# Two-layer encoder trunk on one core: plain products for the first two gate/up tiles of each layer, row sums from rows read back, and moved stores, loads and norms

## The chip, the cores and the metric

The kernel runs on 1 core of one Trainium2 chip. The metric is the device time of one execution in microseconds (us); lower is better. In the profile PE is the matmul engine, PEld its weight loads, DVE the vector engine, ACT the scalar engine, POOL the general engine, SP the engine that issues DMAs in this kernel.

## What is computed

Two layers over x of 1024 rows by 1024 columns in float32. Each layer has a mixer (attention heads and an output projection), a layer norm, a gated feed-forward net of width 2816, and a second layer norm:

```
for layer in range(2):
    mix = mixer(x)                                  # attention, output projection
    x = layer_norm(ALPHA * x + mix, ln1_g, ln1_b)   # over the 1024 columns of a row
    g, u = x @ w_gate, x @ w_up                     # 1024 x 2816 each
    x = layer_norm(ALPHA * x + (silu(g) * u) @ w_down, ln2_g, ln2_b)
```

## The kernel before

Rows are handled in 8 tiles of 128 (`tt`, 0 to 7), features in tiles of 128 on the partitions. Every matmul operand is split into a high and a low part (`split`, L105 on ACT and L106 on DVE, `hilo` calls it), and `mm3` (L127) issues three matmuls for one product of 128x128 by 128x512. So a "product" below, a contraction over 512, is 4 x 3 = 12 matmuls.

The feed-forward net is multiplied in 2x2 blocks by a scheme with 7 block products in place of 8. For gate and up (`gate_up`, 22 tiles `f` of 128 features, taken in pairs `j`, `j + 11`) block row 1 or 2 is gate or up, and the transposed rows give blocks: `b11`, `b21` are the two halves of the columns for rows 0 to 3, `b12`, `b22` those for rows 4 to 7, and `t1` to `t4` are differences of such blocks. On the weight side `prep` builds `s1` to `s4` out of the four loaded blocks `a11` to `a22`. A tile's work is `head` (a11 by b11) and `gate0` (a12 by b21), `m6` (s2 by t2) and `tail` (the other four products). `hidden` stores each tile's result and sums of them to DRAM, and `down_sums` loads four blocks of the down weights, subtracts, and stores four sums. `down` then forms seven products over 11 tiles `j`, each with four banks (`bank_a`: 3 pd and 1 pv; `bank_b`: 2 ps and 2 pt), its operands loaded by `parts` (L430, L431) and split.

What sets the order: a program plans the instruction order of every engine ahead of time from the order of the source, the readiness of operands and a model of durations; the engines then work through their lists in order. The source order is thus a wish. In the result an instruction that waits holds up all behind it on its engine. Tiles come from pools with a fixed number of buffers (g 30, s 3, t 11, wh 6, wr 3, h 6; PSUM pd 3, ps 2, pt 2, pv 1).

Around the change. `out_proj` makes the rows one after another and calls `push` (in `ln_pipe`) for each. `push(tt)` does statistics of row `tt` (L153, L155 on DVE, `rstd` L144 and L146 on POOL), scales the row before (L162 DVE, L163 ACT, times gamma L164 on POOL), adds beta to the row before that (L200 DVE), stores it and calls `turn`. The last two rows take a shorter path (L193, four half-row operations on DVE). In the first norm of a layer `turn` transposes rows 0 to 3 (L235) into b11 and b21 and puts off rows 4 to 7: `sums` (L252) builds b22 and t1 to t4 from the rows in SBUF, called from `gate_up` between four early `head`s that only need b11 and b21. In `down`, rows are loaded again from DRAM (L456) and scaled by ALPHA on ACT (L457) after the first product, `push` for rows 0 to 3 stands behind the fifth product (s2 by t2), and in layer 0 `turn` is `ln_turn` (L172), which transposes rows for the next mixer into PSUM tiles of the same pool `pt` that the sixth product (s3 by t3) takes two of. The last product (a22 by t4) has all 11 operand pairs split first, then runs row by row in the source. SP issues every DMA.

Of the kernel before, what the change touches and what calls it, by code (L numbers as in the profile page):

```python
# [39 lines left out]
class Core:  # L40
# [36 lines left out]
    def w(self):  # L77
        return self.whp.tile([P, 2, WC], F32R, tag="wh", name=self.nm("wh"))

# [78 lines left out]
    def ln_scale(self, y, stats, g):  # L158
# [5 lines left out]
        nc.gpsimd.tensor_tensor(y, y, g, op=ALU.mult)  # L164
# [13 lines left out]
    def ln_pipe(self, y, g, b, turn, done):  # L178
# [3 lines left out]
        n = TT - 2  # L182

        def push(tt):
            if 0 <= tt - 1 < n:
                self.ln_scale(y[tt - 1], st[tt - 1], g)
            if tt < TT:
                st[tt] = self.ln_stats(y[tt])
            if n <= tt < TT:
                mv, r = st[tt]  # L190
                for op, s, row in ((ALU.subtract, mv[:, 0:1], g), (ALU.mult, r, b)):
                    for o in (slice(0, 512), slice(512, D)):
                        nc.vector.scalar_tensor_tensor(y[tt][:, o], y[tt][:, o], s, row[:, o], op0=op,  # L193
                                                       op1=ALU.mult if row is g else ALU.add)
                        if row is b:
                            done(tt, y[tt][:, o], o)
            z = tt - 2
            if 0 <= z < TT:
                if z < n:
                    nc.vector.tensor_tensor(y[z], y[z], b, op=ALU.add)  # L200
                    done(z, y[z])
                if turn is not None:
                    turn(z)
# [37 lines left out]
    def turn_sums(self, y, xb, later):  # L241
        nc = self.nc

        def sums(tt):
            a, b = slice(0, 512), slice(512, D)
            x, z = y[tt - 4], y[tt]
            ta, tb = self.s(), self.s()
            t1, t2, t3, t4 = ta[:, a], ta[:, b], tb[:, a], tb[:, b]
            self.turn_block(xb, "b22", z[:, b], tt)
            for name, o, p, q in (("t1", t1, z[:, a], x[:, a]), ("t2", t2, z[:, b], t1),  # L250
                                  ("t3", t3, z[:, b], z[:, a]), ("t4", t4, x[:, b], t2)):
                nc.vector.tensor_tensor(o, p, q, op=ALU.subtract)  # L252
                self.turn_block(xb, name, o, tt)

        def turn(tt):
            if tt < 4:
                self.turn_block(xb, "b11", y[tt][:, 0:512], tt)
                self.turn_block(xb, "b21", y[tt][:, 512:D], tt)
            else:
                later.append(lambda: sums(tt))  # L260
# [1116 lines left out]
```

## Time and profile before

| | us |
|---|---|
| median of 3 runs | 2545.47 (2544.58 to 2548.05) |
| the profiled execution | 2547.79 |
| its span, first to last instruction | 2546.0 |
| PE busy in it | 2381.7 (94%) |
| DVE busy in it | 1657.1 (65%) |

The stages by time in the span: mixer of layer 0 to about 445 us, its output projection to 491, gate/up to 966, down to 1207; mixer of layer 1 to about 1795, its output projection to 1842, gate/up to 2313, down to 2524, last norm to 2546. A busy share is an average over stages with different limits, so each stage is read for itself. A view by stretches gives the busy time of each engine in a stretch, with the number of its instructions after x, and the clock granted to PE (1.00 is 2.4 GHz, 0.50 is 1.2 GHz).

### The profile page before, as it was taken

Reading aid. Unit: us, or ns where it says so; the run is one execution under the profiler, and the core shown is the slowest. Engines: PE = TensorE matmul, PEld = TensorE weight load, DVE = VectorE, ACT = ScalarE, POOL = GpSimd, SP = SyncE. Lnnn points to the kernel's source line nnn. Section 1 sums busy time; section 2 is a strip of 40 time slices with the busy share of each in tenths; the row PEclk is TensorE's granted clock in tenths of the full one; section 3 lists DMA queues with packets and bytes.
Section 4 is the critical chain, followed back from the end, with each engine's and each line's share of the span. In section 5 each row is a group of like instructions: output and inputs, shape, how many; then the busy total and the mean of one; then the engine's idle time right before and its main releaser. Section 6 shows DMA issues by size and latency. Waiting matters only on the chain.

```text
span 2546.0 us, 35845 instructions
## 1 busy us (share of the span) xinstructions
PE 2381.7 (94%) x11912; PEld 1988.3 (78%) x11912; DVE 1657.1 (65%) x3566; ACT 1123.6 (44%) x2292; POOL 598.0 (23%) x966
## 2 busy tenths in 40 slices
PE   8998999889999999969899999999879999999996
PEld 7977887667888887858688888878758788887885
DVE  3577756868677764566546565656768677764567
ACT  5476756342323325334346665554442232324342
POOL 3532455500000000021344654354600000000012
PEclk9999999989999999979899999999979999999998
DMA  4235232325454469314121212141325544459632
GB/s 155 87 101 158 76 112 65 124 83 180 161 162 157 158 231 360 106 61 176 63 79 42 71 44 63 44 147 53 132 80 176 166 154 161 170 169 378 209 110 86
DMA packets 190906, 337.88 MB, mean 133 GB/s; under 512 B 22392, under 2 KB 48376, under 8 KB 190720
## 3 DMA queue, kind: packets, MB, share of 16 engines
q1 hardware_dynamic: 190720, 335.58, 40.1%
q8 instruction: 95, 1.56, 0.3%
q14 instruction: 91, 0.75, 0.1%
HBM read 236.89 MB, written 94.40 MB: 130 GB/s over the span
## 4 chain that ended last, share of the span: by engine, by line
PE 73%; DVE 12%; DMA 7%; ACT 4%; issue 3%; POOL 2%; SPq 1%; DVEq 0%; ACTq 0%; POOLq 0%
PE pd L127 42%; PE ps L127 12%; PE pt L127 7%; PE pv L689 3%; PE pt L678 3%; PE pv L127 2%; DMA wr<-in_wgu 2%; DVE g L106 2%; DMA g<-in_wd 1%; DVE wh L106 1%; DVE s L650 1%; DVE g L200 1%; PE ps L718 1%; DVE g L193 1%; PE ps L719 1%
## 5 line engine op out<-in xcount | busy, mean ns | idle before, releaser
L127 PE MATMUL pd<-g,wh 128*128 128x512 f32 (+1 forms) x2940 | 738.9, 400 | 31.6 <-ACT g L105 8.1
L127 PEld LDWEIGHTS pd<-g,wh 128*128 128x128 f32 (+1 forms) x2940 | 546.7, 190 | 159.0 <-ACT g L105 9.7
L144 POOL TENSOR_SCALAR m<-m 128x1 f32<-128x1 f32 x32 | 16.8, 525 | 1294.8 <-DVE m L155 1293.3
L106 DVE TENSOR_TENSOR wh<-g,wh 128x1024 fp32r<-128x1024 f32 x138 | 173.3, 1260 | 163.7 <-ACT wh L105 148.8
L105 ACT CAST g<-s 128x512 fp32r<-128x512 f32 x192 | 116.7, 621 | 334.7 <-PE pd L127 147.8
L105 ACT CAST wh<-g 128x1024 fp32r<-128x1024 f32 x138 | 145.0, 1053 | 199.6 <-PE pt L127 63.7
L105 ACT CAST h<-pt 128x512 fp32r<-128x512 f32 (+3 forms) x350 | 157.9, 464 | 138.2 <-PE pt L678 122.4
L106 DVE TENSOR_TENSOR h<-pt,h 128x512 fp32r<-128x512 f32 (+2 forms) x334 | 177.5, 538 | 62.9 <-ACT h L105 60.7
L127 PE MATMUL ps<-g,g 128*128 128x512 f32 (+3 forms) x816 | 201.5, 382 | 8.4 <-DMA g<-kr_scr 4.9
L660 POOL TENSOR_SCALAR s<-s,m 128x128 f32<-128x128 f32 (+1 forms) x192 | 138.3, 722 | 232.1 <-DVE m L659 176.9
L127 PEld LDWEIGHTS ps<-g,g 128*128 128x128 f32 x816 | 147.5, 191 | 37.6 <-DVE m L650 7.3
L127 PE MATMUL pd<-g,g 128*128 128x512 f32 (+2 forms) x756 | 174.4, 376 | 2.2 <-ACT g L105 1.1
L116 POOL TENSOR_TENSOR wh<-wr,wh 128x512 fp32r<-128x512 f32 (+4 forms) x113 | 138.8, 1236 | 150.7 <-ACT wh L115 100.6
L655 ACT ACTIVATE s<-s,m 128x128 f32<-128x128 f32 (+1 forms) x192 | 144.1, 751 | 60.5 <-DVE m L653 50.9
L689 PE MATMUL pv<-h,g 128*128 128x256 f32 x928 | 161.6, 295 | 6.2 <-ACT h L105 2.5
L127 PEld LDWEIGHTS pd<-g,g 128*128 128x128 f32 x756 | 137.2, 190 | 26.0 <-ACT g L105 1.9
L127 PE MATMUL pd<-wh,g 128*128 128x256 f32 (+2 forms) x1056 | 154.1, 294 | 0.0
L106 DVE TENSOR_TENSOR g<-s,g 128x512 fp32r<-128x512 f32 x192 | 131.8, 700 | 33.1 <-ACT g L105 31.0
L689 PEld LDWEIGHTS pv<-h,g 128*128 128x128 f32 x928 | 130.0, 190 | 18.4 <-ACT h L105 7.3
L127 PEld LDWEIGHTS pd<-wh,g 128*128 128x128 f32 x1056 | 142.1, 193 | 1.9 <-DVE g L106 0.3
L678 PE MATMUL pt<-ident,s 128*128 128x128 f32 x816 | 134.0, 276 | 7.2 <-POOL s L660 2.7
L127 PE MATMUL pt<-g,g 128*128 128x512 f32 x528 | 135.0, 393 | 3.5 <-DVE t L383 3.0
(235 smaller groups left out, 4388.1 us busy)
## 6 DMA issues: line engine op xcount, KB each, us to landing
wr<-in_wgu SPq DMA_DIRECT2D x192, 256.0 KB, 2.7
g<-in_wd SPq DMA_DIRECT2D x154, 256.0 KB, 4.1
t<-g SPq DMA_DIRECT2D x88, 256.0 KB, 2.0
s<-t SPq DMA_DIRECT2D x88, 256.0 KB, 2.8
g<-s SPq DMA_DIRECT2D x88, 256.0 KB, 4.5
g<-t SPq DMA_DIRECT2D x88, 256.0 KB, 5.2
a<-t SPq DMA_DIRECT2D x66, 256.0 KB, 2.4
g<-a SPq DMA_DIRECT2D x66, 256.0 KB, 5.3
```

What stands on the lines that cost most here:

```text
L105: self.nc.scalar.copy(hi, src)
L106: self.nc.vector.tensor_tensor(lo, src, fv(hi), op=ALU.subtract)
L116: self.nc.gpsimd.tensor_tensor(hl[:, 1, :], raw, fv(hl[:, 0, :]), op=ALU.subtract)
L127: self.nc.tensor.matmul(out, stat[a], mov[c], start=first and i == 0, stop=last and i == 2, skip_group_check=more)
L193: nc.vector.scalar_tensor_tensor(y[tt][:, o], y[tt][:, o], s, row[:, o], op0=op, op1=ALU.mult if row is g else ALU.add)
L200: nc.vector.tensor_tensor(y[z], y[z], b, op=ALU.add)
L650: nc.vector.tensor_tensor_reduce(out=sb[:, x:y], in0=p, in1=in1, scale=1.0, scalar=m0, op0=ALU.add, op1=ALU.max, accum_out=m)
L655: nc.scalar.activation(sb[:, 0:w], sb[:, 0:w], AF.Exp, bias=neg, scale=scale, accum_out=sm)
L660: nc.gpsimd.tensor_scalar(sb[:, 0:w], sb[:, 0:w], rc, 1.0, op0=ALU.mult, op1=ALU.mult)
L678: nc.tensor.transpose(tp[:, (kb - b0) * P : (kb - b0) * P + P], sb[:, (kb - k0) * P : (kb - k0) * P + P], self.ident)
L689: nc.tensor.matmul(pv, vt(kb), pair[kb // 4][l][:, kb % 4, :], start=c == 0, stop=c == 2 * (last + 1 - first) - 1)
L718: nc.tensor.matmul(p, qt[:, q], kt[:, c : c + w], start=True, stop=False)
```

## The change

The first two tiles of each layer's gate/up are multiplied as 8 plain products each, first for rows 0 to 3 (b11, b21), then for rows 4 to 7 (b12, b22); the four early heads are gone. All rows are transposed into b11 to b22 by `turn`. The sums t1 to t4 for rows 4 to 7 are made in `gate_up` from rows that SP reads back from DRAM, one row pair after each of these steps. Gamma is multiplied on DVE. The stores of `hidden`, of `down_sums` and of the normed rows (but not of the kernel's output) are issued by POOL. In `down` the rows are loaded again one product later, `push` for rows 0 to 3 stands behind the sixth product, and of the last product only the last 4 of 11 operand pairs are split ahead and run row by row; the first 7 run pair by pair. `order` arguments are added and left at their defaults.

```diff
@@ ln_scale
-        nc.gpsimd.tensor_tensor(y, y, g, op=ALU.mult)
+        nc.vector.tensor_tensor(y, y, g, op=ALU.mult)
@@ turn for the first norm, and the sums
-    def turn_sums(self, y, xb, later):
...
+    def turn_blocks(self, y, xb):
         def turn(tt):
-            if tt < 4:
...
+            for i in range(2):
+                self.turn_block(xb, f"b{i + 1}{1 + tt // 4}", y[tt][:, i * 512 : i * 512 + 512], tt)
+    def turn_sums(self, xr_scr, xb, tt):
+        nc = self.nc
+        a, b = slice(0, 512), slice(512, D)
+        x, z = self.s(), self.s()
+        for r, i in ((x, tt - 4), (z, tt)):
+            nc.sync.dma_start(r, xr_scr[i * P : i * P + P, :])
+        t1, t2, t3 = (self.t() for _ in range(3))
+        for name, o, p, q in (("t1", t1, z[:, a], x[:, a]), ("t2", t2, z[:, b], t1),
+                              ("t3", t3, z[:, b], z[:, a]), ("t4", t2, x[:, b], t2)):
+            nc.vector.tensor_tensor(o, p, q, op=ALU.subtract)
+            self.turn_block(xb, name, o, tt)
@@ down_sums and hidden
-                nc.sync.dma_start(o[n], t)
+                nc.gpsimd.dma_start(o[n], t)
-            put = lambda n, t: nc.sync.dma_start(o[n], t)
+            put = lambda n, t: nc.gpsimd.dma_start(o[n], t)
@@ gate_up
-        early = []
-        for i, f in enumerate(order[:heads]):
-            w = {"a11": self.hilo(load(f, 0, 0), self.w()), "a12": self.hilo(load(f, 0, 1), self.w())}
-            p1, u = head(w)
-            early.append((u, gate0(w, p1)))
-            if i >= heads - len(later):
-                later[i - heads + len(later)]()
-        nxt = prep(order[0], dict.fromkeys(("a11", "a12")))
+        def plain(p, w, i, half):
+            b = [f"b{k}{1 + half}" for k in (1, 2)]
+            product(p, w[f"a{i}1"], b[0])
+            product(p, w[f"a{i}2"], b[1], first=False)
+        def plain_half(w, half):
+            p = self.psd()
+            plain(p, w, 1, half)
+            g = self.t()
+            nc.scalar.activation(g, p, AF.Silu)
+            p = self.pss()
+            plain(p, w, 2, half)
+            nc.vector.tensor_tensor(g, p, g, op=ALU.mult)
+            return g
+        pw = [{f"a{i + 1}{j + 1}": self.hilo(load(f, i, j), tile()) for i in range(2) for j in range(2)}
+              for f, tile in zip(order, (self.w, big))]
+        h0 = [plain_half(w, 0) for w in pw]
+        h1 = plain_half(pw[0], 1)
+        self.turn_sums(xr_scr, xb, 4)
+        hidden(order[0], h0[0], h1)
+        self.turn_sums(xr_scr, xb, 5)
+        h1 = plain_half(pw[1], 1)
+        nxt = prep(order[2], {})
+        self.turn_sums(xr_scr, xb, 6)
+        hidden(order[1], h0[1], h1)
+        self.turn_sums(xr_scr, xb, 7)
+        down_sums(0)
         for i, f in enumerate(order):
+            if i < 2:
+                continue
...
@@ down
         product(pa, "a11", "b11")
-        for tt in range(TT):
-            y[tt] = self.g(F32)
-            nc.sync.dma_start(y[tt], xr_scr[tt * P : tt * P + P, :])
-            nc.scalar.mul(y[tt], y[tt], ALPHA)
...
         product(pb, "s1", "t1")
+        for tt in range(TT):
+            y[tt] = self.g(F32)
+            nc.sync.dma_start(y[tt], xr_scr[tt * P : tt * P + P, :])
+            nc.scalar.mul(y[tt], y[tt], ALPHA)
...
+        pb = bank_b()
+        kept = 4
+        homes = iter([self.h() for _ in range(6)] + [self.s().bitcast(F32R), self.g()])
+        product(pb, "s3", "t3")
+        last = [parts(j, "a22", "t4", homes) for j in range(n - kept, n)]
+        for mt in range(4):
             push(mt)
-        pb = bank_b()
-        product(pb, "s3", "t3")
...
-        last = [parts(j, "a22", "t4", homes) for j in range(n)]
         pa = bank_a()
+        product(pa, "a22", "t4", m=n - kept)
         for mt in range(4):
-            for j in range(n):
-                mms(pa[mt], last[j], mt, j == 0, j == n - 1)
+            for j in range(kept):
+                mms(pa[mt], last[j], mt, False, j == kept - 1)
             add(y[4 + mt][:, lo], pa[mt], y[4 + mt][:, lo])
             push(4 + mt)
@@ the stores of both norms' rows, but for the output
-        push = c.ln_pipe(y, lng, lnb, c.turn_sums(y, xb, later), lambda tt, yt, o=slice(0, D), xr_scr=xr_scr: nc.sync.dma_start(xr_scr[tt * P : tt * P + P, o], yt))
+        push = c.ln_pipe(y, lng, lnb, c.turn_blocks(y, xb), lambda tt, yt, o=slice(0, D), xr_scr=xr_scr: nc.gpsimd.dma_start(xr_scr[tt * P : tt * P + P, o], yt))
-            done = lambda tt, yt, o=slice(0, D), x_scr=x_src: nc.sync.dma_start(x_scr[tt * P : tt * P + P, o], yt)
+            done = lambda tt, yt, o=slice(0, D), x_scr=x_src: nc.gpsimd.dma_start(x_scr[tt * P : tt * P + P, o], yt)
```

## Rows read from the trace of the kernel before

**Rows 1.** PE timeline in gate/up: start, us, engine, line, operation, count, idle before.
```profile
657.50 2.88 PE L127 MATMUL ps<-g,g 128*128 128x512 f32 x12
660.22 2.88 PE L127 MATMUL pd<-g,g 128*128 128x512 f32 x12
```

**Rows 2.** Busy time by stretches, gate/up of layer 0 (five) and of layer 1 (three).
```profile
491.00:502.50 11.50, 3.88 (x11) 1.92 (x11) 11.50 (x18) 1.76 (x6) 3.06 (x3) 0.69 0.29 114
502.50:534.70 32.20, 28.84 (x127) 23.32 (x128) 18.05 (x37) 12.51 (x29) 1.69 (x2) 0.90 0.22 74
534.70:550.30 15.60, 7.68 (x40) 6.02 (x38) 11.63 (x26) 8.29 (x21) 0.00 (x0) 0.66 0.12 36
...
600.00:652.00 52.00, 46.89 (x197) 37.73 (x197) 39.74 (x64) 13.41 (x23) 0.00 (x0) 0.97 0.57 189
652.00:966.20 314.20, 313.97 (x1384) 259.41 (x1383) 219.77 (x346) 94.33 (x157) 0.00 (x0) 1.00 0.54 177
...
1842.60:1852.30 9.70, 3.50 (x11) 1.66 (x10) 9.70 (x19) 1.92 (x6) 4.04 (x3) 0.73 0.43 140
1852.30:1883.30 31.00, 28.07 (x126) 22.62 (x127) 16.61 (x34) 12.34 (x28) 1.69 (x2) 0.92 0.23 75
1883.30:1903.00 19.70, 9.54 (x47) 7.24 (x45) 15.72 (x33) 9.85 (x25) 0.00 (x0) 0.62 0.15 43
```

**Rows 3.** The same view: inside down of layer 0, after it, and the end.
```profile
1115.00:1142.50 27.50, 4.47 (x18) 3.00 (x16) 23.37 (x33) 8.63 (x13) 14.10 (x12) 0.59 0.27 97
...
1217.70:1242.00 24.30, 15.29 (x54) 9.17 (x55) 14.35 (x23) 7.05 (x18) 4.52 (x3) 0.65 0.24 86
...
2523.90:2546.00 22.10, 0.36 (x2) 0.00 (x0) 18.04 (x26) 2.37 (x2) 9.58 (x10) 0.55 0.24 95
```

**Rows 4.** Waits of PE: line, who ended the wait: us, times, longest.
```profile
PE pt L235 <- DVE g L106: 21.0, 11, 4.0
PE pt L172 <- DVE g L200: 20.3, 2, 15.1
...
PE pd L127 <- ACT t L371: 5.6, 4, 2.8
```

**Rows 5.** DVE timeline, gate/up of layer 0: a half-row operation, a transposed part.
```profile
545.36 0.69 DVE L288 TENSOR_TENSOR s<-wr,wr 128x512 f32<-128x512 f32 x1 [0.94 <-PE pt L235]
545.96 0.68 DVE L289 TENSOR_TENSOR s<-wr,wr 128x512 f32<-128x512 f32 x1
...
552.28 0.42 DVE L106 TENSOR_TENSOR g<-pt,g 128x256 fp32r<-128x256 f32 x1
```

**Rows 6.** PE timeline, gate/up of layer 0: two transposed blocks.
```profile
526.13 0.60 PE L235 MATMUL pt<-ident,s 128*128 128x128 f32 x4
526.57 0.60 PE L235 MATMUL pt<-ident,g 128*128 128x128 f32 x4
```

**Rows 7.** Gamma (L164) and beta (L200): duration min/median/max in ns, first and last start.
```profile
L164 POOL TENSOR_TENSOR g<-g,b x24: 2345/2417/3382, 461.7 to 2535.7; 128x1024 f32<-128x1024 f32 x24
...
L200 DVE TENSOR_TENSOR g<-g,b x24: 1208/1216/3415, 464.7 to 2540.7; 128x1024 f32<-128x1024 f32 x24
```

**Rows 8.** PE timeline at the start of down in layer 0, and SP there.
```profile
971.48 0.97 PE L127 MATMUL pd<-wh 128*128 128x512 f32 x3 [2.12 <-ACT wh L105]
...
958.37 4.22 SPq L456 DMA_DIRECT2D g<-xr_scr  x8
```

**Rows 9.** DVE timeline of the last norm, layer 1.
```profile
2522.94 1.29 DVE L425 TENSOR_TENSOR g<-pd,g 128x512 f32<-128x512 f32 x2 [7.79 <-PE pd L127]
...
2530.11 9.56 DVE L193 SCALAR_TENSOR_TENSOR g<-g,m,b 128x512 f32<-128x512 f32 x8
2539.59 2.35 DVE L200 TENSOR_TENSOR g<-g,b 128x1024 f32<-128x1024 f32 x2
```

**Rows 10.** Timelines: a short POOL instruction (last norm), a store issued by SP (gate/up).
```profile
2486.53 1.54 POOL L146 TENSOR_TENSOR m<-m,mhalf 128x1 f32<-128x1 f32 x1
...
575.24 0.33 SPq L329 DMA_DIRECT2D t<-g  x1
```

More of the change, by code (lines that the diff above doesn't have):

```diff
@@ L176, in ln_turn, with ln_pipe @@
                 self.split(hi, lo, p[:, k * 256 : k * 256 + 256].rearrange("p (k c) -> p k c", k=2))
-    def ln_pipe(self, y, g, b, turn, done):
+    def ln_pipe(self, y, g, b, turn, done, order=range(TT)):
         st = {}
@@ L239, in turn_block, with turn, ffn @@
             self.split(hi[k][:, :, o], lo[k][:, :, o], p[:, k * 256 : k * 256 + 256].rearrange("p (k c) -> p k c", k=2))
-    def turn_sums(self, y, xb, later):
-        nc = self.nc
[L244 to L255, printed above, removed]
-            if tt < 4:
[L257 to L260, printed above, removed]
-        return turn
-    def ffn(self, xb, y, xr_scr, wgu, wd, lng, lnb, turn_next, done, later, scr):
+    def turn_blocks(self, y, xb):
+        def turn(tt):
+            for i in range(2):
+                self.turn_block(xb, f"b{i + 1}{1 + tt // 4}", y[tt][:, i * 512 : i * 512 + 512], tt)
+        return turn
+    def turn_sums(self, xr_scr, xb, tt):
+        nc = self.nc
+        a, b = slice(0, 512), slice(512, D)
[7 more added lines that the diff above has]
+            self.turn_block(xb, name, o, tt)
+    def ffn(self, xb, y, xr_scr, wgu, wd, lng, lnb, turn_next, done, scr):
         half = NF // 2
@@ L308, in prep @@
             a12 = load(f, 0, 1)
-            if "a12" not in w:
-                w["a12"] = self.hilo(a12, self.w())
+            w["a12"] = self.hilo(a12, self.w())
             w["s3"] = self.hilo(sb, big())
@@ L431, in parts @@
             nc.sync.dma_start(raw[:, hi], ops[j][b])
-            if homes is None:
-                h, l = (self.w().rearrange("p s c -> p (s c)") for _ in range(2))
-            else:
-                h, l = next(homes), next(homes)
+            h, l = (next(homes) if homes else self.wflat() for _ in range(2))
             self.split(h, l, raw)
@@ L442, in mms, with product @@
             self.mm3(p, (h[:, c], l[:, c]), (h[:, hi], l[:, hi]), first, last, more)
-        def product(p, a, b, first=True):
-            for j in range(n):
+        def product(p, a, b, first=True, m=n):
+            for j in range(m):
                 op = parts(j, a, b)
@@ L595, in out_weights, with out_proj @@
         return ws
-    def out_proj(self, o_scr, x_src, ws, kts, y, push=None, more=None):
+    def out_proj(self, o_scr, x_src, ws, kts, y, push=None, more=None, order=tuple(range(TT))):
         nc = self.nc
         load = lambda tt: self.weight(o_scr[tt, :, kts[0] : kts[-1] + 1, :].rearrange("p k c -> p (k c)"), 512)
-        nxt = load(0)
+        nxt = load(order[0])
         if more is not None:
             ws = ws + more()
-        for tt in range(TT):
-            oh, nxt = nxt, load(tt + 1) if tt + 1 < TT else None
+        for z, tt in enumerate(order):
+            oh, nxt = nxt, load(order[z + 1]) if z + 1 < TT else None
             if x_src is not None:
```

60 lines of the change are left out of this document (27 added, 33 removed).

## The prediction

> **What bounds the kernel now.** I read the stretches first. In the long middle of gate/up PE is busy 313.97 of 314.2 us and DVE 219.77 [rows 2]: there PE is the bound, one instruction goes by every 314.2 / 1384 = 0.227 us, and a product of twelve matmuls takes 2.72 us from start to start [rows 1]. Nothing that only relieves DVE, SP or the DMA queues is worth time there. The time that can be had lies where PE is idle: the begin of gate/up [rows 2], one hole in down of layer 0, the hand-over to the next mixer, and the last norm [rows 3]. The waits of PE name DVE for the two longest sums: transposes (L235) behind a low part, and two transposes of `ln_turn` (L172) behind beta, 15.1 us the longest [rows 4]. So I cost the change hole by hole.
>
> **Added work of PE.** Two tiles get 8 products in place of 7: 2 x 2.72 = 5.4 us a layer. Rows 4 to 7 are also transposed into b12 (b22 was made before): 4 blocks of four transposes, 0.44 us from start to start (0.11 us each) [rows 6], 1.8 us. Together 7.2 us a layer, **+14.4 us**, all on PE and so all on the path.
>
> **Begin of gate/up.** Before: the early heads are 8 products, 96 matmuls, of which 3 run in the first stretch (11 instructions, 8 of them transposes) and 93 from 502.5 to 550.3 us [rows 2]. These cost 93 x 0.227 = 21.1 us, the other 74 instructions are transposes, 8.1 us; the stretch has 47.8 us, so 18.6 us are lost, the clock (0.66 after the heads) included. From 600 to 652 us 197 instructions should take 44.7 us and take 52.0: 7.3 us lost. In layer 1, from 1852.3 to 1903, it is 50.7 - 21.1 - 80 x 0.11 = 20.8 us. Lost in all: 46.7 us. After the heads of before PE has nothing but transposes whose sources DVE makes one by one.
>
> After: PE has 4 + 4 products for rows 0 to 3 (21.8 us, the same length as the old heads) and then 8 more for rows 4 to 7, which need no differences. Beside these last 21.8 us, 64 transposes (7.0 us) and the next head (5.4 us), 34 us, DVE has for t1 to t4 16 x (0.60 + 2 x 0.33) = 20.2 us, 11 half-row operations of `prep` (6.6 us), and 12 for gating, `hidden` and `down_sums` (7.2 us): 34 us, by starts 0.60 us apart for a half row and 0.33 for a 256-wide low part [rows 5]. Balanced, so PE should wait little but not never. I leave per layer the loss of the like-balanced stretch at 600 to 652 us (7.3 us, DVE busy 39.74 of 52.00) and one wait for the first Silu, 2.8 us as the longest such wait [rows 4]: 10 us. Gain 46.7 - 20 = **-27 us**; bounds 0 (DVE no sooner) and -41 (only the Silu's wait stays).
>
> The reads back (8 of 512 KB a layer) replace 8 loads of 256 KB of the heads; DMA share there is 0.12 to 0.29 [rows 2], so they are covered as long as rows 0 to 3's 21.8 us of products run. A read waits on SP for POOL's store of its row; behind it on SP queue the weight loads of `prep`, and PE waits for those. If that cover fails it costs inside the 0-bound.
>
> The gap before the first head (11.5 and 9.7 us, DVE busy all of it [rows 2]) I leave as it is. Gamma adds 6 x about 1.13 us to DVE in each norm (as beta, 1.208 us alone [rows 7]), but the sums leave this stretch, and POOL's `rstd` no longer queues behind a gamma of 2.4 us. Bounds -4 to +8 us a layer.
>
> **Gamma beside POOL.** Beta on DVE takes 1.208 us at best and 3.415 at worst, gamma on POOL 2.345 to 3.382 [rows 7]: the two stretch each other. With gamma on DVE that is gone; it is counted in the norms below.
>
> **Start of down.** Before, eight reads of rows go out on SP ahead of the second product's loads, ACT scales eight rows between splits, and PE waits 2.12 us for a split once [rows 8]. Later reads move this collision to where operands are already ahead. I take -2 us a layer, **-4 us**; bounds 0 and -9 (waits and slow restart, twice).
>
> **The hole in down, layer 0.** 27.5 us with 4.47 us of PE work at clock 0.59 [rows 3]: the sixth product takes its two `pt` banks after the transposes of rows 0 and 1, and these wait for statistics, scale, gamma and beta. After, the banks are taken first, and the norm of rows 0 to 3 has the whole sixth product, 11 x 2.72 = 30 us, as cover. DVE needs for the norm of four rows 4 x (1.2 statistics + 1.13 gamma + 1.13 beta + 0.2) = 14.6 us there beside a low part of 1.2 us in every 2.72: it fits. If the cover fails, splits come late and PE waits inside the product. The 16 transposes themselves remain (1.8 us) and I leave 2 us for a wait on them: **-24 us**; bounds -27.5 and -10.
>
> **Hand-over to the mixer of layer 1.** 24.3 us hold 54 instructions worth about 9 us [rows 3], so 15 are lost while DVE works off the norm of four rows that all end at once. After, the last four pairs run row by row: rows 4, 5 and 6 end 8.2, 5.4 and 2.7 us before row 7. I take **-7 us**; bounds 0 (the order planned mixes the rows again) and -12.
>
> **The last norm.** From the last matmul to the end 22.1 us [rows 3], of which DVE runs from 2522.94 to 2541.94, with eight L193 in 9.56 us, 1.2 us each, beside POOL's gamma [rows 9]. After: adds 2.4, statistics 4.8, small 0.7, gamma 2.3, L193 8 x 0.62 = 5.0, beta 2.3, in all 17.5 us, begun 8.2 us earlier but with some idle time before row 7: about 11 us after the last matmul in place of 19. **-8 us**; bounds -3 and -12.
>
> **Stores on POOL.** The trace of before shows no DMA issued by POOL. Per pair of tiles (14 products, 38.1 us) there are 11 stores. Nearest rows: SP issues one in 0.33 us; a short POOL operation beside DVE took 1.54 us; a full one up to 3.38 us [rows 7, 10]. At 3.38 the queue has 37.2 of 38.1 us: it still keeps pace, and nothing waits for a store but the buffers of `t` and the row reads. What is queued behind a store on POOL is the next row's `rstd`, and DVE's L162 waits for that; before, gamma's 2.4 us stood there. I take 0; bounds -2 (SP's loads no longer behind stores at the begin) and the rival below.
>
> The Trainium skill speaks against this edit. "SBUF — State Buffer", section "SBUF: two separate sides", says that such DMAs have their descriptors written by the general engine, which the vector engine can lock out, and advises to issue them elsewhere; the section "A bandwidth-pool intuition that's wrong" gives 3.1 us for one that takes 0.62 alone. By an estimate from that page 11 x 3.1 = 34 us of 38.1 would go to stores: late, but in pace, so the sum would stay. No run here shows it yet.
>
> **The sum.** 14.4 - 27 - 4 - 24 - 7 - 8 = -55.6 us against the profiled execution: 2547.8 - 55.6 = 2492.2. The median lies 2.3 us below that execution, so **2490 us**. Taking half of each bound's distance (they won't all go one way) the case spans about 2465 to 2520.
>
> **The rivals.**
> - *The begin stays bound by DVE* (its 34 us run in an order planned ahead, and each wait there holds the rest up). For it: DVE was busy all of the gap before the heads. Against it: PE now has 21.8 us of products that need no DVE. Gain 0 there: 2490 + 27 = 2517. Chance 0.15.
> - *The order planned is not the source's.* The change doesn't do what it says in down: the transposes still stand before the sixth product, as the last product of before ran mixed although its source goes row by row. 2490 + 24 + 8 = 2522. Chance 0.08.
> - *All holes close to their far bounds.* 14.4 - 41 - 9 - 27.5 - 12 - 12 = -87.1: 2458. Chance 0.08.
> - *Slower: stores on POOL hold up DVE in all of gate/up.* DVE has 30% idle in the long middle [rows 2], 11.4 us per pair. If each store blocks DVE for X, DVE becomes the bound from X = 1.04 us, and the 56 us are eaten at (11 X - 11.4) x 20 pairs = 56, X = 1.3 us. At the 1.54 us of the short operation [rows 10] it adds 111 us: 2601. For it: beta and gamma stretch each other. Against it: what SP does for a store is over in 0.33 us, and no engine is held up beside it. Chance 0.07.
>
> **How the numbers follow.** The forecast has 0.62. The range 2450 to 2525 takes in the forecast's span and the first three rivals and leaves out the slower one and a little of each edge. A measurement of this kernel can tell some 0.2%, 5 us, from no change. Faster by more: 0.90; within: 0.03 (the first two rivals together, 2549); slower: 0.07.
>
> **What would show it.** Right: no PE gap over 10 us in down of layer 0; PE on products without a break over 5 us from the first plain product to the main loop, at clock near 1; the last operation of DVE about 11 us after the last matmul; 222 matmuls per 50 us in the long middle as before. Wrong: DVE busy above 90% or PE gaps in the long middle (stores); transposes L172 ahead of the sixth product's matmuls; the four rows of the last product ending together; PE waiting for t1 to t4 or for row reads; a longer gap between the output projection and the first plain product (gamma).

## The result, and the profile after

The change takes the kernel from 2545.98 us (median of 4 runs, 2544.58 to 2548.05) to **2500.4 us** (median of 4 runs, 2496.34 to 2502.68), a ratio of 0.9819 with a 95% interval of 0.9802 to 0.9836. The forecast was 2490, in a range of 2450 to 2525. The profiled execution after took 2500.94 us with a span of 2499.1, so 46.9 us left the span where the sum of the forecast had 55.6.

To compare stages between kernels I cut every trace at the same events: a stage of gate/up ends with the last multiplication by a Silu on DVE, down with the last addition of a bank on DVE, the hand-over with PE's first 8-row transpose of the next mixer. Lengths in us (the medians are of all runs of a kernel, the stages of its profiled run, which in e8_down_gamma was 5.7 us over the median and elsewhere nearer; the runs e1 to e13 are told below):

| kernel | median | to end of gate/up, layer 0 | down 0 | hand-over | mixer 1 to end of gate/up 1 | down 1 | last norm |
|---|---|---|---|---|---|---|---|
| before | 2546.0 | 969.6 | 238.8 | 51.4 | 1058.0 | 208.3 | 20.1 |
| after | 2500.4 | 966.5 | 219.8 | 43.1 | 1052.0 | 205.7 | 11.9 |
| e1_down | 2522.2 | 967.1 | 230.9 | 42.4 | 1054.8 | 214.7 | 11.6 |
| e8_down_gamma | 2508.0 | 968.9 | 224.8 | 44.2 | 1054.1 | 207.6 | 12.2 |
| e2_begin | 2550.0 | 971.6 | 237.9 | 50.7 | 1059.2 | 206.6 | 19.6 |
| e4_gamma_pool | 2528.7 | 973.9 | 226.8 | 45.2 | 1057.4 | 213.2 | 11.7 |
| e3_stores_sp | 2503.1 | 963.9 | 223.6 | 44.2 | 1051.0 | 208.1 | 11.9 |
| e13_push_back | 2512.4 | 964.4 | 231.6 | 41.8 | 1055.0 | 205.7 | 11.9 |
| e5_spread | 2487.8 | 956.6 | 220.9 | 44.3 | 1046.8 | 205.7 | 12.0 |
| e6_push_late | 2490.0 | 964.5 | 209.3 | 44.1 | 1050.6 | 205.7 | 11.9 |
| e9_in_place | 2479.9 | 960.3 | 209.2 | 45.0 | 1044.4 | 205.7 | 11.9 |
| e10_bank | 2452.6 | 946.6 | 209.2 | 44.5 | 1034.2 | 205.7 | 11.9 |
| e11_bank_reads | **2436.0** | 937.0 | 209.3 | 45.1 | 1025.8 | 205.7 | 12.0 |
| e12_gu_sp | 2443.5 | 939.1 | 211.9 | 44.2 | 1025.7 | 206.2 | 12.2 |

Down, the hand-over and the last norm gained about what was forecast. Gate/up, where the largest term stood, gained next to nothing: from PE's last operation ahead of the gap before the first product it took 478.6 us in layer 0 and 474.6 in layer 1 before, and 474.9 and 477.4 after.

The page of after, engine totals, and then its view by stretches (length; busy us and count of PE, PEld, DVE, ACT, POOL; clock granted to PE; DMA share; GB/s). The lines answer [rows 2] and [rows 3].

```profile
PE 2375.3 (95%) x11992; PEld 1992.3 (80%) x11992; DVE 1625.5 (65%) x3558; ACT 1118.5 (45%) x2292; POOL 678.3 (27%) x1214
```

```profile
491.50:498.90 7.40, 1.68 (x10) 1.65 (x9) 7.40 (x14) 1.12 (x3) 1.35 (x3) 0.81 0.74 242
499.00:553.60 54.60, 54.55 (x258) 44.53 (x256) 27.00 (x54) 16.80 (x39) 4.62 (x9) 0.96 0.33 113
553.60:581.90 28.30, 11.45 (x49) 8.96 (x49) 24.94 (x49) 13.37 (x32) 4.32 (x8) 0.64 0.63 213
600.00:964.90 364.90, 364.67 (x1609) 301.58 (x1607) 255.54 (x402) 104.70 (x179) 57.36 (x106) 1.00 0.52 179
1109.50:1139.50 30.00, 29.62 (x131) 24.23 (x130) 28.95 (x41) 13.82 (x13) 6.36 (x11) 1.00 0.32 110
1139.50:1153.50 14.00, 6.44 (x31) 4.40 (x29) 11.25 (x22) 4.22 (x11) 0.53 (x1) 0.69 0.19 75
...
1867.70:1896.80 29.10, 13.97 (x54) 10.17 (x52) 25.57 (x50) 13.34 (x32) 4.32 (x8) 0.59 0.61 210
2486.00:2499.10 13.10, 0.17 (x1) 0.00 (x0) 10.17 (x17) 0.23 (x1) 2.25 (x4) 0.64 0.40 160
```

Read them in turn. The plain products run without a break (54.55 of 54.6 us). Behind them stands a new hole, 28.3 us with 11.45 us of PE work in layer 0 and 29.1 with 13.97 in layer 1, at a clock of about 0.6. From 553.11 to 575.86 us PE has no product at all, only transposes, where the forecast wanted products without a break over 5 us. The long middle is as full as before. The sixth product in down runs through (29.62 of 30.0), but 14.0 us with 6.44 us of work come behind it. After the last matmul 13.1 us remain, in place of 22.1.

PE's waits of the whole run after, which answer [rows 4]:

```profile
PE pt L240 <- DVE g L109: 44.4, 14, 7.9
...
PE pt L175 <- DVE g L109: 6.9, 3, 4.8
```

L240 is the transpose of a block, L109 the low part of a split (line numbers differ between kernels: they are L235 and L106 in before; gamma is L164 there and L167 in the others, beta L200, then L203 or L205; the transpose of `ln_turn` L172, then L175). And the timeline (start, us, engine, line, operation, count, idle before) of DVE, of PE and of SP where the new hole begins to form:

```profile
529.70 0.68 DVE L263 TENSOR_TENSOR t<-s 128x512 f32<-128x512 f32 x1
540.04 0.69 DVE L410 TENSOR_TENSOR t<-ps,t 128x512 f32<-128x512 f32 x1 [9.66 <-PE ps L130]
...
537.04 2.89 PE L130 MATMUL ps<-h,wh 128*128 128x512 f32 x12
539.77 1.04 PE L240 MATMUL pt<-ident,t 128*128 128x128 f32 x8
...
530.41 14.14 SPq L259 DMA_DIRECT2D s<-xr_scr  x2
```

The first differences (L263) were ready at 530.4. PE transposed them at 539.77, since in its list they stand behind the half product of the first tile for rows 4 to 7. DVE had nothing to do for 9.66 us, and the reads of the next rows (L259) waited for the buffers of `s`. So of the 21.8 us of products that I had counted as cover for the sums, half was not used.

### The profile page after: what moved, and what is told of

Same layout as the page of the kernel before. It is cut to its first block, busy times and chain, and to the rows that moved or that the text cites. A ratio compares the mean times of both kernels' runs of the same rounds, so it can differ in the third digit from the quotient of the medians.

```text
span 2499.1 us, 36064 instructions
## 1 busy us (share of the span) xinstructions
PE 2375.3 (95%) x11992; PEld 1992.3 (80%) x11992; DVE 1625.5 (65%) x3558; ACT 1118.5 (45%) x2292; POOL 678.3 (27%) x1214
## 4 chain that ended last, share of the span: by engine, by line
PE 79%; DVE 9%; DMA 4%; issue 4%; ACT 2%; POOL 1%; SPq 0%; DVEq 0%; POOLq 0%; ACTq 0%
PE pd L130 45%; PE ps L130 14%; PE pt L130 7%; PE pv L705 3%; PE pt L694 3%; PE pv L130 2%; DVE g L109 1%; DMA wr<-o_scr 1%; DVE s L666 1%; PE ps L734 1%; PE ps L735 1%; DVE st L156 1%; DVE g L205 1%; DVE wh L109 1%; DVE g L167 1%
## 5 line engine op out<-in xcount | busy, mean ns | idle before, releaser
L130 PE MATMUL pd<-g,wh 128*128 128x512 f32 (+1 forms) x2916 | 731.1, 400 | 15.3 <-ACT g L108 6.6
L109 DVE TENSOR_TENSOR wh<-g,wh 128x1024 fp32r<-128x1024 f32 x146 | 177.4, 1224 | 140.8 <-ACT wh L108 111.9
L108 ACT CAST g<-s 128x512 fp32r<-128x512 f32 x176 | 107.1, 621 | 328.1 <-PE pd L130 155.0
L108 ACT CAST wh<-g 128x1024 fp32r<-128x1024 f32 x146 | 153.1, 1053 | 184.7 <-PE pt L130 62.1
L109 DVE TENSOR_TENSOR h<-pt,h 128x512 fp32r<-128x512 f32 (+2 forms) x334 | 177.6, 538 | 67.8 <-ACT h L108 65.5
L130 PE MATMUL ps<-g,g 128*128 128x512 f32 (+3 forms) x840 | 206.2, 381 | 8.5 <-DMA g<-kr_scr 5.1
L335 POOL DMA_DIRECT2D a<-t x66 | 35.7, 541 | 550.5 <-DVE t L390 401.6
L130 PE MATMUL pd<-g,g 128*128 128x512 f32 (+2 forms) x744 | 168.2, 372 | 0.3 <-ACT g L108 0.3
L130 PEld LDWEIGHTS pd<-g,g 128*128 128x128 f32 x744 | 133.2, 188 | 21.8 <-ACT g L108 0.7
L109 DVE TENSOR_TENSOR g<-s,g 128x512 fp32r<-128x512 f32 x176 | 121.7, 704 | 33.6 <-ACT g L108 31.9
L130 PE MATMUL pd<-wh,wh 128*128 128x512 f32 x480 | 124.4, 391 | 0.3 <-DVE wh L109 0.2
```

The source lines that it names most:

```text
L108: self.nc.scalar.copy(hi, src)
L109: self.nc.vector.tensor_tensor(lo, src, fv(hi), op=ALU.subtract)
L130: self.nc.tensor.matmul(out, stat[a], mov[c], start=first and i == 0, stop=last and i == 2, skip_group_check=more)
L335: put = lambda n, t: nc.gpsimd.dma_start(o[n], t)
```

## The experiments

**The two halves of the change.** First down alone, in the kernel before:

```diff
 # kernel before
-            push(mt)
...
         product(pb, "s3", "t3")
+        last = [parts(j, "a22", "t4", homes) for j in range(n - kept, n)]
+        for mt in range(4):
+            push(mt)
...
-        last = [parts(j, "a22", "t4", homes) for j in range(n)]
+        product(pa, "a22", "t4", m=n - kept)
```

> The kernel before with the changes in down alone: rows reloaded one product later, the norm of rows 0 to 3 behind the sixth product, 4 of 11 operand pairs kept for the last product. Theory: nearly all that the change gained comes from here. By the traces of before and after: down of layer 0 -20 us, hand-over to the next mixer -9, down of layer 1 -4, last norm -6 (a little less than the 9 of after, since gamma stays on POOL), mixer of layer 1 -8 if its new order comes from the hand-over: 2546 - 47 = about 2500, the same as after within 6 us. Rival A (the begin of gate/up did gain what I forecast, and the gain was eaten elsewhere): then this kernel keeps before's begin and lands 12 us or more above after, 2512 or more. Rival B (the 8 us in the mixer come from somewhere else, stores or gamma): 2508, with the mixer of layer 1 at before's 582 us.

(The diff is cut: the later reload of the rows and the 4 kept pairs are in it too.) Measured: 2522.2, ratio 0.9904 (0.9879 to 0.993), 22 us over the expected 2500. The hand-over and the last norm gained all that they gain in after (42.4 and 11.6 us), but down of layer 0 only 7.9 us, and down of layer 1 lost 6.4. Rival A's number fits and its reason doesn't: gate/up did not gain in after. What was missing is in down of layer 0 of this run, by stretches and then in the timeline of DVE:

```profile
1130.00:1140.00 10.00, 9.38 (x42) 7.44 (x40) 9.26 (x5) 6.29 (x6) 10.00 (x6) 1.00 0.13 52
```

```profile
1130.90 2.36 DVE L165 SCALAR_TENSOR_TENSOR m<-m,m 128x1 f32<-128x1 f32 x1 [0.35 <-POOL m L149]
...
1134.32 6.75 DVE L203 TENSOR_TENSOR g<-g,b 128x1024 f32<-128x1024 f32 x2
1141.00 4.49 DVE L109 TENSOR_TENSOR wh<-g,wh 128x1024 fp32r<-128x1024 f32 x2
```

```profile
1130.84 12.43 POOL L167 TENSOR_TENSOR g<-g,b 128x1024 f32<-128x1024 f32 x4
...
1144.41 2.07 PE L130 MATMUL ps<-wh,wh 128*128 128x512 f32 x4 [5.03 <-DVE wh L109]
```

L203 is beta: two take 6.75 us, 3.4 each, where one takes 1.2 alone [rows 7]. Two splits take 4.49, the second of them behind the last gamma, and an operation on one column 2.36. POOL is busy all of the 10 us with the norm's gammas; they are stretched too, four in 12.43 us where one takes 2.4. DVE gets five operations done, the splits of the sixth product stand among them, and PE waits 5.03 us for one.

Then the begin of gate/up alone:

```diff
 # after, with down of before, and
-        nc.vector.tensor_tensor(y, y, g, op=ALU.mult)
+        nc.gpsimd.tensor_tensor(y, y, g, op=ALU.mult)
-    put = lambda n, t: nc.gpsimd.dma_start(o[n], t)      # and the other stores
+    put = lambda n, t: nc.sync.dma_start(o[n], t)
```

> The other half: the change without its edits in down, and with stores back on SP and gamma back on POOL, so that only the begin of gate/up (plain products, sums from rows read back) differs from before. Theory: the begin is worth nothing, because the stall after the plain products (28 us in each layer) took the place of the holes of before: 2546 +- 5. Rival A (the begin gains 12.6 us net as I forecast and POOL stores or gamma on DVE ate it): 2533, with no stall over 10 us between the plain products and the main loop. In both, the hole of some 27 us in down of layer 0 is there as in before.

Measured: 2550.0, ratio 1.0019 (1.0006 to 1.0032), and down of layer 0 has its old length (237.9 us). The begin by itself is worth nothing, as the theory said (it costs 4 us, and the interval leaves out no change); rival A falls.

**Gamma, twice.** Added to the first run, and taken from after:

```diff
 # e8: e1_down with      # e4: after with the reverse
-        nc.gpsimd.tensor_tensor(y, y, g, op=ALU.mult)
+        nc.vector.tensor_tensor(y, y, g, op=ALU.mult)
```

> The first run with the changes in down alone (2522, not the 2500 I expected) plus gamma on DVE. In its trace five DVE operations fill 9.26 of 10 us of the sixth product in layer 0 (1130 to 1140 us) while POOL is busy all 10, and PE then stands still. New theory: gamma on POOL is the partner without which moving the norm gains only part, because beta and the splits beside it take up to 3.4 us. With gamma on DVE: down of layer 0 -11, down of layer 1 -9 (both to after's length), 2500 to 2504, the same as after within 4 us. Rival F (the stores on POOL are the partner): nothing changes, 2518 to 2524. For the mixer of layer 1 the theory says nothing; if gamma's place decides its order too, its stage is 577 us as in after, otherwise 586.

> After with gamma back on POOL. Theory (gamma is the partner of the moved norm): some 20 us slower than after, 2515 to 2525, with the loss in both down stages (about 10 each) and in the stretch before the first plain product (1 to 4 each). Rival F (stores are the partner): 2500 to 2506. My forecast had put gamma at nothing by itself in the first norm, bounds -4 to +8 a layer, and had no price for it in down.

Measured: e8 2508.0, ratio 0.984 (0.9816 to 0.9864); e4 2528.7, ratio 0.9917 (0.9895 to 0.9939). Both end 4 us over the range expected of them: in e8 down of layer 0 gained 6.1 us over e1 and not 11, down of layer 1 7.1 and not 9. What after has beyond e8 is the new begin and the stores on POOL. Gamma's place is worth 14 us beside the begin and stores of before and 28 beside those of after. In after's company gamma on POOL costs 7.0 and 7.5 us in the two down stages, 2.1 in the hand-over and some 13 in the stages up to the end of gate/up, the norms beside the output projections and the mixer of layer 1 among them. Rival F falls: the stores are not the partner. With gamma on DVE the same place of the timeline reads, in e8:

```profile
1133.07 1.22 DVE L167 TENSOR_TENSOR g<-g,b 128x1024 f32<-128x1024 f32 x1
...
1141.09 2.35 DVE L109 TENSOR_TENSOR wh<-g,wh 128x1024 fp32r<-128x1024 f32 x2
```

Gamma and each split take 1.2 us. The Trainium skill has the rule, "SBUF — State Buffer", section "Who interferes with whom": a DVE instruction with two SBUF inputs contends with a GpSimd instruction that reads SBUF, and the contention is an exclusive lock, not a sharing of bandwidth. The trace agrees: the 2.36 us of the one-column operation are about the length of one whole gamma on POOL (2.417 [rows 7]).

**The stores.**

```diff
 # after
-                nc.gpsimd.dma_start(o[n], t)       # down_sums; likewise hidden, rows of both norms
+                nc.sync.dma_start(o[n], t)
```

> After with all its stores issued by SP again. Theory: nothing in the long middle, where PE is the bound; in the begin the row reads and weight loads queue behind stores on SP that wait for data, 0 to 3 us a layer: 2500 to 2506, the same as after or just over 0.2% slower. Rival F (stores on POOL are the partner of the moved norm, or set the mixer's order): 2512 or more, with down or the mixer of layer 1 longer by 8 us and more. [...]

Measured: 2503.1, ratio 0.9818 (0.9799 to 0.9837), the same as after, as the theory said. The prediction's slower rival, stores on POOL that hold up DVE, falls on the durations. The half-row operations of DVE in the long middle of gate/up, in after and then in this run (count, busy us, mean ns):

```profile
L109 DVE TENSOR_TENSOR g<-s,g 128x512 fp32r<-128x512 f32 x68 | 46.1, 688 | 7.7 <-ACT g L108 7.0
```

```profile
L109 DVE TENSOR_TENSOR g<-s,g 128x512 fp32r<-128x512 f32 x68 | 45.9, 685 | 8.1 <-ACT g L108 7.4
```

They are 3 ns apart, with 106 POOL instructions in the long middle of after. A store holds POOL for 541 ns on the mean:

```profile
L335 POOL DMA_DIRECT2D a<-t x66 | 35.7, 541 | 550.5 <-DVE t L390 401.6 <-DVE t L394 79.4 <-DVE t L410 56.5
```

**The hole in down, by itself.**

```diff
 # after
             add(y[mt][:, hi], u[mt], y[mt][:, hi])
+            push(mt)
         pb = bank_b()
...
-        for mt in range(4):
-            push(mt)
```

> After with one thing undone: the norm's steps for rows 0 to 3 in down stand ahead of the sixth product again; late reload of the rows, 4 kept pairs, gamma on DVE and all else stay. This prices the hole in down of layer 0 by itself. Theory (my forecast: the banks of the sixth product wait behind the transposes of rows 0 and 1, 24 us, of which gamma on DVE now gives a part in any case, 6 to 7 us by the run with gamma on POOL): down of layer 0 is 13 to 20 us longer than after's 220, the whole 2513 to 2520. Rival H (with gamma on DVE the norm is quick enough wherever it stands): less than 5 us, 2500 to 2505.

Measured: 2512.4, ratio 0.9868 (0.9848 to 0.9889); down of layer 0 is 11.8 us longer than after's. That is a little under the theory's 13 to 20, and well over rival H's 5. PE stands before the transposes of rows 0 and 1 as in [rows 4]:

```profile
1120.54 1.97 PE L175 MATMUL pt<-ident,g 128*128 128x128 f32 x8 [12.53 <-DVE g L205]
```

So, each taken out of after alone, the place of the norm is worth 11.8 of the 19.0 us that down of layer 0 gained, and gamma on DVE 7.0. They are not shares that add: with SP issuing the stores (e3) it is 3.8 us longer too, and both together on the kernel before (e8) gave 14.0.

**The stall that was left in down.**

```diff
 # after
-        for mt in range(4):
+        for mt in range(2):
             push(mt)
...
         product(pa, "a22", "t4", m=n - kept)
+        for mt in range(2, 4):
+            push(mt)
```

> After, with the norm's steps for rows 2 and 3 (in layer 0 with the transposes of rows 0 and 1) put behind the first 7 pairs of the last product instead of ahead of it. Theory: of the 14-us stall between the sixth and the last product in layer 0 (6.44 us of PE work) 6 to 7 us come back: 2493 to 2495. Rival E (DVE is what is late, and the transposes move to where the last rows already press on it): the hand-over to the mixer grows by what the stall loses, 2500 +- 3, and the last norm of layer 1 grows by 1 to 3 us.

Measured: 2490.0, ratio 0.9781 (0.9751 to 0.9811). Down of layer 0 is 10.5 us shorter, the hand-over 1.0 longer, the last norm the same; the whole is 3 us better than expected. PE now works through behind the sixth product:

```profile
1137.00:1160.00 23.00, 23.00 (x111) 19.20 (x110) 17.88 (x26) 10.66 (x17) 5.85 (x7) 1.00 0.21 70
```

Rival E falls. The gain exceeds the 7.6 us of idle time; the clock granted there is 1.00 in place of 0.69.

**The hole after the plain products, step by step.** First the order:

```diff
 # after
-        h1 = plain_half(pw[0], 1)
-        self.turn_sums(xr_scr, xb, 4)
-        hidden(order[0], h0[0], h1)
-        self.turn_sums(xr_scr, xb, 5)
-        h1 = plain_half(pw[1], 1)
+        sums(4)
+        h1[1] = plain_half(pw[1], 1, lambda: sums(5))   # between its two products
+        sums(6)
+        h1[0] = plain_half(pw[0], 1, lambda: sums(7))
```

> After, with the sums of the four row pairs put between the plain products of rows 4 to 7 instead of behind them, the second tile's products (whose weights lie in g) ahead of the first one's, t4 in a tile of its own, and the sums of the first down tile two steps later. Theory: the stall (28.3 and 29.1 us with 11.5 and 14.0 us of PE work, clock about 0.6) is a matter of order: the sums wait behind products in PE's list and the next rows' reads wait for the sums; with PE work beside them 8 to 12 us per layer come back, 2500 - 20 = 2480 (2475 to 2487). Rival C (DVE's work, 34 us by my estimate, is the bound of the begin in any order): the same stall or the same loss elsewhere before 600 us, 2500 +- 5. Rival D (the reads back and the buffers of s are the bound): the stall is shorter by less than half, 2490 to 2495, and PE's waits end behind L263 that waits for DMA.

Measured: 2487.8, ratio 0.9774 (0.9747 to 0.9801): 12.6 us of the 20, just outside the range. PE's waits of L240 for L109 behind the plain products of layer 0 fell from 16.9 us in all to 9.1. But in the rest of the hole DVE was full:

```profile
553.00:565.00 12.00, 3.51 (x17) 2.59 (x17) 12.00 (x24) 6.59 (x15) 1.09 (x2) 0.67 0.40 130
```

That looked like rival C, the amount of DVE's work. The next run joined this with the step in down and took the buffers of `t` out of the way:

```diff
 # e5_spread with the pushes of e6_push_late, and in turn_sums
-        t1, t2, t3, t4 = (self.t() for _ in range(4))
+        xa, xc, za, zc = x[:, 0:512], x[:, 512:D], z[:, 0:512], z[:, 512:D]
+        for o, p, q in ((xa, za, xa), (za, zc, za), (zc, zc, xa), (xc, xc, zc)):
+            nc.vector.tensor_tensor(o, p, q, op=ALU.subtract)
```

> Both improvements joined and one step further: the spread sums with their four subtractions made in place in the two read-back tiles (no tile of t is needed, and the next row's reads wait for transposes alone), the sums of rows 4 and 5 ahead of the first product of rows 4 to 7, and the norm's steps of rows 2 and 3 in down behind the first 7 pairs. Theory (order and buffers, not DVE's amount of work, set the rest of the begin's stall): the two earlier gains add, 12.2 + 10.0 us, and 2 to 4 us more per layer come back: 2500.4 - 22 - 6 = 2472 (2466 to 2478). Rival C (DVE is at its limit from 540 to 567 us, where it was busy all the time): only the two gains add, 2478 or a little more, and DVE is still busy without a break for 20 us after the plain products.

Measured: 2479.9, ratio 0.9729 (0.9711 to 0.9748), above the expected range: the two gains add (12.6 + 10.4 gives 2477.4), the step beyond them brought nothing. Rival C has the number, but not the reason, because DVE is not full in what is left of the hole (15.06 of 20.00 us):

```profile
485.00:500.00 15.00, 9.28 (x43) 7.12 (x41) 15.00 (x29) 4.23 (x9) 4.40 (x8) 0.80 0.62 199
...
550.00:570.00 20.00, 11.07 (x48) 7.88 (x47) 15.06 (x31) 7.70 (x19) 2.17 (x4) 0.72 0.45 146
```

The same kernel's timeline follows one turned block from PE through its two rounds of ACT (high part) and DVE (low part):

```profile
551.91 0.60 PE L240 MATMUL pt<-ident,s 128*128 128x128 f32 x4
552.54 0.37 ACT L108 CAST g<-pt 128x256 fp32r<-128x256 f32 x1 [3.77 <-PE pt L240]
552.95 0.42 DVE L109 TENSOR_TENSOR g<-pt,g 128x256 fp32r<-128x256 f32 x1 [3.72 <-ACT g L108]
553.40 0.37 ACT L108 CAST g<-pt 128x256 fp32r<-128x256 f32 x1 [0.49 <-DVE g L109]
553.88 0.41 DVE L109 TENSOR_TENSOR g<-pt,g 128x256 fp32r<-128x256 f32 x1
```

From 551.91 to 554.29 a block holds its PSUM bank, 2.4 us, and `pt` has two. PE, ACT and DVE each have gaps in it: none of them is the limit, the round trip is. The bank `pv` stands idle in this stage, which gives the test:

```diff
 # e9_in_place, turn_block
-        p = self.pst()
+        self.turned = getattr(self, "turned", 0) + 1
+        p = self.psv() if self.turned % 3 == 0 else self.pst()
```

> The last version (2479.9) with every third transposed block in the begin put into the PSUM bank pv, which stands idle there, beside the two of pt. In that version the stall after the plain products is down to about 16 us with 7 us of PE work, and DVE is no longer full in it (15.06 of 20 us from 550 to 570), so the amount of DVE work is not what is left. Theory (banks: a block holds its bank for the transposes and two rounds of ACT and DVE, some 2 us, and two banks let PE turn one block about every 1 us at most, less with every wait of ACT for DVE): 3 to 6 us per layer, 2468 to 2474. Rival D (what is left is the chain of reads and the buffers of s: the next row's reads wait until the last block of the row before is turned): 2477 to 2482. Rival C (DVE's amount): 2480.

Measured: 2452.6, ratio 0.9634 (0.9615 to 0.9653): 27 us, more than the theory's 6 to 12, with the same operations on every engine. Rivals C and D, which left nothing for a bank, fall as they stand. PE's idle time ahead of the transposes of the begin, over both layers, was 44.4 us in after (above) and 32.6 in e5. In e9 and then in this run it is ("issue" means that the profile names no releaser):

```profile
PE pt L240 <- DVE g L109: 16.0, 4, 8.1
PE pt L240 <- issue: 14.4, 6, 2.8
```

```profile
PE pt L241 <- issue: 7.2, 2, 4.0
```

In the next run there is none. By stretches, this run:

```profile
485.00:500.00 15.00, 15.00 (x75) 12.43 (x74) 15.00 (x30) 6.27 (x13) 3.82 (x7) 1.00 0.59 210
540.00:550.00 10.00, 8.24 (x44) 6.50 (x42) 6.61 (x14) 3.90 (x10) 0.00 (x0) 1.00 0.34 109
550.00:560.00 10.00, 6.20 (x20) 4.57 (x20) 10.00 (x20) 4.95 (x12) 1.63 (x3) 0.56 0.45 157
```

The first line is the surprise. The gap ahead of the first plain product is gone too, PE 15.00 of 15.00 us where it was 9.28, and DVE has 15.00 in both. DVE was busy all of that gap, and yet it was not the bound: with a third bank the transposes of the early rows get ahead, and PE has products while DVE works off the later rows. (The bank also changed the planned order, so the gain is that of the bank with the order that it allows.)

```diff
 # e10_bank, turn_sums
-        x, z = self.s(), self.s()
+        if tt in (4, 6):
+            xa, xc, za, zc = (self.t() for _ in range(4))    # read as half rows into t
+        else:
+            x, z = self.s(), self.s()
```

> The same with the third bank, and the rows of pairs 4 and 6 read back into four half tiles of t, which are free there, so that three of the four row pairs can be read before any sum is turned. Theory (banks and reads each hold a part): 2 to 5 us more per layer than the third bank alone, 2460 to 2470. Rival (banks alone): the same as the third bank alone within 3 us. Rival D (reads alone): this one is the first to gain, 2468 to 2474, and the third bank alone had nothing.

Measured: **2436.0**, ratio 0.9569 (0.9551 to 0.9586), 16.6 us under the third bank alone and over the 4 to 10 expected. All the reads are half rows of 256 KB in it, also those into `s`. Banks and reads each held a part; reads without the third bank were not tried. The hole of [rows 2] and of after is closed:

```profile
485.00:500.00 15.00, 15.00 (x75) 12.42 (x74) 15.00 (x30) 6.28 (x13) 3.81 (x7) 1.00 0.43 158
540.00:550.00 10.00, 9.34 (x50) 7.67 (x49) 10.00 (x21) 6.78 (x17) 0.00 (x0) 1.00 0.35 105
550.00:560.00 10.00, 10.00 (x51) 8.36 (x50) 10.00 (x22) 6.11 (x15) 2.17 (x4) 1.00 0.53 182
```

Here DVE is full from 540 to 560 us, and PE is not kept waiting. This version beats both kernels, 110 us under before and 64 under after.

```diff
 # e11_bank_reads, down_sums and hidden only
-                nc.gpsimd.dma_start(o[n], t)
+                nc.sync.dma_start(o[n], t)
```

> The one before with the stores of gate/up (tiles and the sums of the down weights) issued by SP again, those of the normed rows still by POOL. With all stores on SP the run was 2.7 us slower than after, but by stages gate/up was 1.3 and 3.7 us shorter and down 3.8 and 2.4 us longer. Theory (stores on POOL help in down, where SP would wait with the loads behind them, and cost a little in gate/up): 2 to 5 us faster than the one before. Rival (stage differences of that size are the order planned anew, not the queue): within 2 us either way, and which sign is chance.

Measured: 2443.5, ratio 0.9596 (0.9578 to 0.9613): 7 us slower than the one before (2441.22 to 2444.67 against 2435.23 to 2437.86), the other way than my theory; the stage differences from which I had drawn it did not carry it. One place shows a cause. With SP issuing, the last tile's stores stand in its queue among the first loads of down, and the reads of the rows go out at 950.94 us, 5.3 later than in e11. ACT waits for the first of them and is late with the splits behind it, for one of which PE waits; in e11 neither wait is there:

```profile
955.59 1.06 ACT L484 ACTIVATE g<-g 128x1024 f32<-128x1024 f32 x1 [5.09 <-DMA g<-xr_scr]
...
970.50 0.73 PE L130 MATMUL ps<-wh 128*128 128x512 f32 x2 [1.31 <-ACT wh L108]
```

The rest of the 7 us is not located.

## Why the prediction was right, and where not

The time came out 10 us over the forecast and inside its range, and by the mechanism named for down, the hand-over and the last norm. That it came so near is in part luck: the begin of gate/up fell 11.7 us short, and the mixer of layer 1, which had no term, gave 8.8. In the order of its parts, predicted and measured in the span:

| part | predicted | measured |
|---|---|---|
| gate/up of both layers (added work 14.4, begin -27) | -12.6 | -0.9 |
| both down stages (start -4, hole -24) | -28 | -21.6 |
| hand-over | -7 | -8.3 |
| last norm | -8 | -8.2 |
| mixer and output projection of layer 1 | no term | -8.8 |

(The rows add up to 47.8 us; gate/up of layer 0 begins 0.6 us later than before, and the rest of the difference to 46.9 is rounding.)

- **Added work of PE** was right: 80 more instructions by the two pages, 48 matmuls and 32 transposes, which makes 14.4 us at the durations used; the cost was not measured by itself.
- **Begin of gate/up** is the step that failed. With 14.4 us of work added and 0.9 gained, the holes gave back 15.3 us and not 27. The step set DVE's 34 us against PE's 34 us and took the result as balanced. Two things were wrong in it. The 21.8 us of products are cover only for what the lists of the engines put beside them, and the source puts the first sums behind half of them (e5: 12.6 us). And the wait of PE for L106 in [rows 4], 21.0 us, was read as a lack of sources. L106 reads the bank and writes the block, it makes no source of a transpose: that wait is for the release of a bank. A third bank, with the order that it allows, was worth 27 us in e10 without one operation less. The Trainium skill, "Perfetto Trace Analysis", section "Optimization Strategy", names too few buffers in PSUM as one thing that a recurring gap can mean; e10 agrees. The rival of a begin bound by DVE came half true in its size, and not in its reason: with the third bank and the reads DVE is full from 540 to 560 us and PE still has work. For the kernel before its row points the same way, but no run tried it.
- **The gap before the first product** was left at 0, because DVE was busy all of it. By the stretches it changed from 11.5 to 7.4 us in layer 0 and stayed near 10 in layer 1, inside the bounds. But its reading fell, as e10 shows.
- **The hole in down** closed by 19.0 us for -24 with a part of the -4: what was missing is the 14.0-us stall behind the sixth product, for which I had left 2 us. The norm did fit beside the sixth product, as the step had it (DVE 28.95 of 30 us), but the transposes of rows 0 and 1 come next in PE's list, ahead of the last product, and wait 7.3 us in all: 1.82 for additions that read the sixth product's banks of `pt`, 4.83 and 0.68 for L109. Both are again releases of a bank. e6 brought back 10.5 us by moving the later steps of the norm with these transposes. I had also counted the place of the norm as the whole cause. Taken out of after alone it is worth 11.8 us, gamma on DVE 7.0; without gamma on DVE the edits in down are worth 7.9 in layer 0 and cost 6.4 in layer 1 (e1).
- **Gamma** had its price in the last norm and in the gap before the first product, but none in down. By e4 it is worth 28 us in after, half of them in the two down stages.
- **Start of down**: the 2.12-us wait of [rows 8] is gone. Down of layer 1, which has no hole, is 2.6 us shorter; -2 a layer was forecast, but e4 puts gamma alone at 7.5 there, so this is not shown to be the wait's share.
- **Hand-over and last norm** were right in mechanism and size. The last rows now end one after another, and DVE ends 10 us after the last matmul (11 was forecast). e1 has both gains with gamma still on POOL, and e13 keeps both with the norm's steps put back, so of the edits in down the row-by-row end is left, or the late reload, which was not taken out alone. The 1.2 us for one of the eight L193 of [rows 9] are a mean: six of the eight took some 0.75 us, and two beside a gamma 2.8. Over all 32 in the kernel (min/median/max in ns), before and after:

```profile
L193 DVE SCALAR_TENSOR_TENSOR g<-g,m,b x32: 733/747/2885, 493.1 to 2538.9; 128x512 f32<-128x512 f32 x32
```

```profile
L198 DVE SCALAR_TENSOR_TENSOR g<-g,m,b x32: 703/748/751, 495.4 to 2495.4; 128x512 f32<-128x512 f32 x32
```

- **Stores on POOL** at 0: e3 can't be told from after, and the slower rival falls with DVE's 688 against 685 ns. The rule of the Trainium skill quoted against the edit, "SBUF — State Buffer", section "A bandwidth-pool intuition that's wrong", does not show here: POOL's issue takes 0.54 us beside a busy DVE, not some 3. Its 3.1 us are for a DMA beside a `tensor_copy` on DVE, and in the long middle DVE has only two-input TENSOR_TENSOR operations, so the two don't contradict each other. Landing is 0.4 to 0.7 us later than from SP by the pages of after and before (3.2, 2.4 and 3.1 us in place of 2.8, 2.0 and 2.4). In the last version POOL is the better issuer by 7 us, more than the -2 of my bound.
- **The mixer of layer 1**, with its output projection, went from 583.4 to 574.6 us and had no term. Nothing in the mixer's own source was changed, only the norm beside its output projection (gamma, stores, transposes). Cut at the last attention product, 4.9 us of the 8.8 lie ahead of it. Over all kernels here in which it can be cut off it lies between 573.8 and 583.4, also where only the begin or only down was changed (578.2 and 579.1). The order planned for it differs each time. Which part of that order matters was not tried.

## What to carry to other kernels

A wait names who ended it, not what was missing: where an engine that writes a PSUM tile waits for an operation that only reads such a tile, the tile's buffer is short, and neither engine's busy share will tell. Count a product as cover only if the work to be covered stands beside it in the lists of the engines. And when a step is moved to where an engine is busy, price its partners on the shared path (here gamma on POOL beside splits on DVE) at that place.

## What was not expected of the hardware

- Beside multiplications of 128x1024 on POOL (2.4 us alone, four in 12.43 here), a DVE operation on a single column took 2.36 us, two betas 6.75, and two splits, one of them after the last multiplication, 4.49; alone, splits and betas take 1.2 each.
- A store issued by POOL held that engine for 0.54 us on the mean in each of three groups (88, 88 and 66 stores), and left DVE's operations at 0.69 us.
- A stall can cost more than its idle time: in the holes of after (14.0 to 29.1 us long, PE busy about half of them) the granted clock was 0.59 to 0.69, and closing the one of 14.0 us, with 7.6 us idle, gave 10.5.
